# Three instead of two attention-output jobs behind the attention heads, in a single-core decoder block on Trainium2

## The chip, the cores and the metric

The kernel runs on one core of a Trainium2 chip. The metric is the device time of one execution, in microseconds (us), given as the median of several runs. The engines are named as in the profile: PE does matrix products, PEld loads their weights, DVE, ACT and POOL are the vector, scalar and general-purpose engines, SP issues most of the transfers.

## The reference

One decoder block over 2048 tokens of width 1024, in float32. What the change touches is the attention branch's output, its merge with the recurrent branch, and the last projection:

```python
h = rms_norm(x, g_norm[l]) * (1.0 + scale[:, None, :]) + shift[:, None, :]
proj = h @ w_in[l]
x_rnn, z_rnn, q, k, v, z_attn, g_r, g_a = jnp.split(proj, IN_SPLITS, axis=-1)
...
y_rnn = (hr * jax.nn.silu(z_rnn.astype(jnp.float32))).astype(dt) @ w_out_rnn[l]
...
o = dilated_attention_mixture(qh, kh, vh).reshape(B, S, D_ATTN)
y_attn = (o * jax.nn.silu(z_attn.astype(jnp.float32))).astype(dt) @ w_out_attn[l]
merged = jax.nn.sigmoid(g_r + bg_r) * y_rnn + jax.nn.sigmoid(g_a + bg_a) * y_attn
x = x + gate[:, None, :] * (merged @ w_o[l])
return rms_norm(x, g_final)
```

There are 8 heads of 128 channels. Attention is the mixture of three causal windows with dilations 1, 4 and 16.

## The kernel before

All products are made of pairs of float32r operands: a number is split into a high part (a copy, on ACT, `hi_act`) and a low part (the difference, on POOL or DVE, `lo_pool` and `lo_dve`), and `mm3` issues three matmuls for each product (high by high, high by low, low by high). The work goes through these stages:

1. The input projection and the recurrent branch, for the two halves of the sequence. Nothing of it changes. At its end the output weights are written to memory, once as split pairs (`wD`) and, for the attention weights, once unsplit (`wR`).
2. Attention. The sequence has four banks of 512 tokens. There are 16 "heads": the 8 heads for the first two banks, then the 8 heads for the last two. Each head has six units (`ORDER`), and one slot takes one unit through the engines by a written-out order (`plan`, `at`, `run`): scores of the slot's unit, softmax, and, seven slots later, transposes, and another slot later the sums with the values. A slot's work on the other engines is the softmax with its scaling (ACT and DVE), the splits of keys, queries, values (ACT high, POOL low) and of the transposed weights (ACT or DVE high, DVE low).
3. Between the parts of each slot a generator, `steps`, is advanced by `spend`. It makes the output products as eight jobs of 64 steps: jobs 0 to 3 multiply the recurrent branch (`yaT`) for banks 0 to 3, jobs 4 to 7 the attention branch (`oT`) for banks 0 to 3. A job has eight tiles (m), a tile has eight steps (k), and a step is one `mm3` on a 128x512 tile `pj`. How many steps a slot takes is `FILL`: 3.6 in the first half of the slots and 3.1 in the second, with `MORE` (0.8) in seven early slots. What is left after the last slot is issued at once.
4. The tail: the jobs at tile index `TAIL0` and above run behind the attention heads. Here the weights come unsplit from `wR` and are split as they come (`split_w`, high on ACT, low on DVE and POOL in turn); the first two halves still come as pairs. Beside these jobs `build_rows` makes the operands of the last projection from `w_o`, in four builds (k = 0 to 3), each at a written-out step of the tail: load two row blocks into the stage tiles st1 and st2, scale them with the gate (`gate_rows`, POOL), form the sums of a Strassen product (`combine`, DVE), and split them (`high` on ACT, `low` on DVE or POOL).
5. The last projection: eight pairs of seven products each, then the final norm. Its first pair reads only bank 0.

Each job's right-hand operand Y (eight 128x512 blocks) is loaded (`load_y`) into a ring of four R tiles and split (`split_y`) into yh and yl, nine of each, at steps given by `LOAD_Y` and `SPLIT_Y`. These count from the boundary of the jobs: step x belongs to the last tile of the job before for x = 0 to 7, and to the first tile of the job itself from 8 on, so that block k is needed at x = 8 + k. Each tile's result is multiplied with its merge gate, in jobs 4 to 7 added to the recurrent result, and stored (`load_g`, `evict`, `store`). The load of gates has a ring of four fg tiles, and every third tile of the tail uses s1 and s2.

With TAIL0 = 48 two jobs, 6 and 7, are in the tail. Job 6 reads bank 2, which the last heads write; its last block is taken from the last head's own tile, and three others through spare key tiles:

```python
if ys is oT and (n, k) == (2, KT - 1):
    Y0[False, n, k] = last_head[0].zt[:, 0].rearrange("p r j -> p (r j)")
    return
if ys is oT and n == 2 and k >= KH:
    t = T(ap_, [P, KQW], F32, "kraw", bufs=4)
    nc.sync.dma_start(t[:, :CH], ys[k * P : (k + 1) * P, n * CH : (n + 1) * CH])
    Y0[False, n, k] = t[:, :CH]
    return
```

Engines take their instructions in the order of the program, and so does each queue of transfers.

Of the kernel before, what the change touches and what calls it, by code (L numbers as in the profile page):

```python
# [10 lines left out]
F32 = mybir.dt.float32  # L11
# [9 lines left out]
P = 128  # L21
S = 2048
D = 1024
KT = D // P
NB = 4
CH = 512
# [5 lines left out]
BIG = 9984.0  # L32


FILL = (3.6, 3.1)
MORE = 0.8
NEG = 1e30

# [51 lines left out]
def decoder_block(ctx, tc, x, c, positions, g_norm, w_mod, b_mod, w_in, b_gate, conv_w, conv_b,  # L90
# [4 lines left out]
    def T(pool, shape, dt, tag, **kw):  # L95
        cnt[0] += 1
        return pool.tile(shape, dt, tag=tag, name=f"{tag}_{cnt[0]}", **kw)
# [1553 lines left out]
            at(e + 2, TAIL, self.store)  # L1651

    stored = set()
    TAIL0 = KT * (NB + 2)
    RAW = 2 * TAIL0 + 1


    def steps(jobs):

        tiles = [(j, m) for j in range(len(jobs)) for m in range(KT)]  # L1660
        Y, G = {}, {}

        def load_w(x):

            if x < 2 * len(tiles):
                assert x == n_w[0]
                j, m = tiles[x // 2]
                if x <= RAW:
                    load_wd(jobs[j][0], m, x % 2)
                    return  # L1670

                n_w[0] += 1
                i = (x - 2 * TAIL0) % 6
                W[x] = t = T(pS, [P, 2, KH, P], F32R, f"S{i}") if i < 4 else T(fp, [P, 2, KH, P], F32R, f"st{i - 1}")
                nc.sync.dma_start(t[:, 1].bitcast(F32), wR[m, x % 2])

        def split_w(x):
            if RAW < x < 2 * len(tiles):
                raw = W[x][:, 1].bitcast(F32)
                hi_act(W[x][:, 0], raw)  # L1680
                (lo_pool if x % 2 else lo_dve)(W[x][:, 1], raw, W[x][:, 0])

        def load_y(j, k):
            if j < len(jobs):
                w, ys, n = jobs[j]
                if ys is oT and (n, k) == (2, KT - 1):

                    Y0[False, n, k] = last_head[0].zt[:, 0].rearrange("p r j -> p (r j)")
                    return
                if ys is oT and n == 2 and k >= KH:  # L1690

                    t = T(ap_, [P, KQW], F32, "kraw", bufs=4)
                    nc.sync.dma_start(t[:, :CH], ys[k * P : (k + 1) * P, n * CH : (n + 1) * CH])
                    Y0[False, n, k] = t[:, :CH]
                    return
                assert ys is yaT or (n // 2, k, n % 2) in stored
                load_yd(ys, n, k)

        def split_y(j, k):
            if j < len(jobs):  # L1700
                Y[j, k] = yh, yl = [T(fl, [P, CH], F32R, tag, bufs=NY) for tag in ("yh", "yl")]
                w, ys, n = jobs[j]
                t = Y0.pop((ys is yaT, n, k))
                hi_act(yh[:], t[:])
                (lo_dve if k % 2 else lo_pool)(yl[:], t[:], yh[:])

        def load_g(t):
            j, m = tiles[t]
            w, ys, n = jobs[j]
            at_ = slice(m * P, (m + 1) * P), slice(n * CH, (n + 1) * CH)  # L1710
            G[t] = []
            for src in (grT,) if ys is yaT else (gaT, mrT):
                if t >= TAIL0 and (t - TAIL0) % 3 == 2 and t < TAIL0 + 13:
                    g = T(fp, [P, CH], F32, ("s1", "s2")[len(G[t])])
                else:
                    g = T(fl, [P, CH], F32, "fg", bufs=4)
                nc.sync.dma_start(g[:], src[at_])
                G[t].append(g)

        def evict(t, ps):  # L1720
            g = G[t]
            nc.vector.tensor_tensor(g[0][:], ps[:], g[0][:], ALU.mult)  # L1722
            if len(g) > 1:
                nc.vector.tensor_tensor(g[0][:], g[0][:], g[1][:], ALU.add)

        def store(t):
            j, m = tiles[t]
            w, ys, n = jobs[j]
            nc.sync.dma_start((mrT if ys is yaT else meT)[m * P : (m + 1) * P, n * CH : (n + 1) * CH], G.pop(t)[0][:])

        g_loads = {(0, 0): [0], (14, 0): [14], (15, 0): [15]}
        for x in range(13):
            g_loads[x, 3] = [x + 1]
        for k in range(KT):
            split_y(0, k)
        yield
        last = None
        for t, (j, m) in enumerate(tiles):
            ps = T(pj, [P, CH], F32, "pj")
            for k in range(KT):  # L1740
                x = 2 * t + k // KH
                if k % KH == 1:

                    if x < 2 * TAIL0:
                        load_w(x + 3)
                    for x1 in range(x + 3 if x == 2 * TAIL0 else x + 5, x + 6) if x >= 2 * TAIL0 else ():
                        load_w(x1)
                if k % KH == 2 and x >= 2 * TAIL0:
                    for x1 in (x + 2, x + 3) if x == 2 * TAIL0 + 1 else (x + 2,) if x == 2 * TAIL0 else (x + 3,):
                        split_w(x1)  # L1750
                if k == 1 and t:
                    evict(t - 1, last)
                if t < TAIL0:
                    if k == 3:
                        load_g(t)
                    if k == 7 and t:
                        store(t - 1)
                else:
                    if k == 4:
                        store(t - 1)  # L1760
                    for x in g_loads.pop((t - TAIL0, k), ()):
                        load_g(TAIL0 + x)
                wt = W[2 * t + k // KH]
                yh, yl = Y[j, k]
                mm3(ps[:], wt[:, 0, k % KH, :], wt[:, 1, k % KH, :], yh[:], yl[:], first=k == 0, last=k == KT - 1)
                if k % KH == KH - 1:
                    W.pop(2 * t + k // KH)


                x = m * KT + k - KT * (KT - 1)  # L1770
                j1 = j + 1
                if m == 0:
                    x, j1 = x + KT * KT, j

                if j1 == NB + 2:

                    if -14 <= x < KT - 14:
                        load_y(j1, x + 14)
                elif j1 and x in LOAD_Y:
                    load_y(j1, LOAD_Y[x])  # L1780
                if j1 and x in SPLIT_Y:
                    split_y(j1, SPLIT_Y[x])
                yield
            last = ps
        evict(len(tiles) - 1, last)
        store(len(tiles) - 1)
# [12 lines left out]
    LOAD_Y = {-12: 0, -10: 1, -8: 2, -6: 3, -2: 4, 4: 5, 5: 6, 6: 7}  # L1799
    SPLIT_Y = {-3: 0, 3: 1, 4: 2, 5: 3, 7: 4, 10: 5, 11: 6, 12: 7}  # L1800
    fill = steps([(0, yaT, n) for n in range(NB)] + [(1, oT, n) for n in range(NB)])
    next(fill)
    with tc.manual_schedule():
        units = []
        for g in range(2 * H):
            hd = Head(g // H, g % H)
            hd.enlist(NU * g)
            units += [(hd, u) for u in ORDER]
        last_head = [hd]
        owed = 0.0  # L1810
        first = min(s for s, _ in plan)
        end = max(s for s, _ in plan) + 1
        for s in range(first, max(end, len(units) + LAG + 1)):
# [22 lines left out]
                if evict:  # L1836
                    at(s + 1, HEAD, evict)
            run(s, TAIL)
        owed = spend(fill, (NB + 2) * KT * KT - n_steps[0], 0)
    pools.close("ap", "sc", "pT", "po")  # L1840

    fp = pools.open("fp", bufs=1)
# [9 lines left out]
    def on(n, fn, *args):  # L1852
        pend.setdefault(n, []).append((fn, args))
# [29 lines left out]
    def build_rows(s, k):  # L1883
        sub, add = ALU.subtract, ALU.add
        for d, fn, *args in (
            (0, gate_rows, k, 0), (4, gate_rows, k, 1), (5, high, "B11", k), (6, low, "B11", k, lo_dve),
            (9, combine, "T3", k, "B22", "B12", sub), (9, combine, "T2", k, "B11", "T3", add),
            (9, high, "B22", k), (9, high, "B21", k), (10, low, "B22", k, lo_pool), (10, low, "B21", k, lo_dve),
            (11, high, "T3", k), (11, high, "T2", k), (12, combine, "T4", k, "B21", "T2", sub), (12, low, "T3", k, lo_pool),
            (13, low, "T2", k, lo_dve), (13, high, "T4", k), (14, combine, "T1", k, "B22", "T2", sub),  # L1890
            (15, high, "T1", k), (15, low, "T4", k, lo_dve), (16, low, "T1", k, lo_pool)):
            on(s + d, fn, *args)

    A, ops = {}, {}
# [167 lines left out]
        on_p(n + 3, finish_row, p, 1)  # L2062
        fire_p()

    LAST = 2 * KT * KT
    with tc.manual_schedule():
        v["gate"] = stage(0, [P, D])
        nc.sync.dma_start(v["gate"][:], gateD[0:1, :].broadcast_to([P, D]))
        for k, x in enumerate((8, 32, 68, 92)):
            build_rows(x, k)  # L2070
            for i in range(2):
                on(max(x - 8 + 4 * i, 0), load_rows, k, i)
        on(107, load_left, 0, (0,))
# [58 lines left out]
```

## Time and profile before

| | |
|---|---|
| Median of 3 runs | 2251.11 us (2250.35 to 2255.52) |
| The profiled execution's own time | 2251.41 us |
| Its span, first to last instruction | 2249.6 us |
| Busy share of the span: PE, PEld, DVE, ACT, POOL | 97%, 82%, 64%, 57%, 48% |
| Mean granted PE clock | 0.988 |
| Memory traffic | 577.34 MB by transfers, mean 257 GB/s |

The span is shorter than the execution's time by 1.8 us. Busy time of PE counts a matmul from its start to its modelled end, which overlaps the next one, so that 97% is no measure of how densely it works; the distance between the starts of two matmuls is. The granted clock is 1.0 or 0.5 in any one moment, and a mean between them tells for what share of a stretch it was halved. Idle time of an engine is shown with what ended it.

### The profile page before, as it was taken

To read this page: it belongs to the slowest core of one execution; us is meant where nothing else is said; L and a number is where in the kernel's file an instruction comes from. 1 tells how busy PE (TensorE), PEld (TensorE's weight loads), DVE (VectorE), ACT (ScalarE), POOL (GpSimd) and SP (SyncE) were. 2 spreads that over 40 slices of the span, in tenths; PEclk is the share of its full clock that TensorE was granted. 3 is DMA by queue.
4 is the path that set the end of the run, shared out by engine and by line. 5 is a ranking of instruction groups with operands and counts; after the bars stand their busy time and mean duration, and the time that the engine had idled before them with its cause. 6 is when DMAs were issued, how large, how long until landed. Compare 5 with 4: busy or idle time off the path is not lost. (4 is left out here: it accounts for less than half of the span.)

```text
span 2249.6 us, 34130 instructions
## 1 busy us (share of the span) xinstructions
PE 2176.6 (97%) x11326; PEld 1840.2 (82%) x11326; DVE 1441.9 (64%) x2467; ACT 1282.6 (57%) x2554; POOL 1084.3 (48%) x799
## 2 busy tenths in 40 slices
PE   8999999999999999999999999999999998978998
PEld 4998888888778988888888877888888887856886
DVE  5838887878445815545445442566667776678787
ACT  5637678667533627556556203676778877433333
POOL 2557777767557422222222102555656655366443
PEclk9999999999999999999999999999999999988999
DMA  8367887887999378898999989988988877877543
GB/s 276 114 220 255 285 292 270 293 283 263 324 279 292 108 234 278 273 298 288 292 306 296 358 291 292 276 273 250 280 255 259 253 239 228 265 230 221 201 164 113
DMA packets 412133, 577.34 MB, mean 257 GB/s; under 512 B 72406, under 2 KB 270258, under 8 KB 410932
## 3 DMA queue, kind: packets, MB, share of 16 engines
q1 hardware_dynamic: 369748, 446.75, 63.9%
q10 hardware_dynamic: 42016, 128.36, 15.0%
q8 instruction: 90, 1.47, 0.3%
q14 instruction: 87, 0.71, 0.1%
q0 software_dynamic: 192, 0.05, 0.0%
HBM read 356.92 MB, written 218.11 MB: 256 GB/s over the span
## 5 line engine op out<-in xcount | busy, mean ns | idle before, releaser
L150 PE MATMUL pj<-yh,S 128*128 128x512 f32 x944 | 347.1, 410 | 22.6 <-DVE s L1722 6.5
L164 POOL TENSOR_TENSOR S<-R,S 128x512 fp32r<-128x512 f32 x168 | 256.8, 1536 | 175.1 <-ACT S L158 72.2
L150 PE MATMUL X<-T,S 128*128 128x512 f32 x1344 | 326.0, 392 | 5.0 <-ACT u L384 4.3
L150 PE MATMUL V<-T,S 128*128 128x512 f32 x1344 | 324.5, 390 | 1.2 <-DVE t L454 0.9
L150 PEld LDWEIGHTS X<-T,S 128*128 128x128 f32 x1344 | 252.8, 189 | 59.9 <-ACT u L384 5.5
L150 PEld LDWEIGHTS V<-T,S 128*128 128x128 f32 x1344 | 252.0, 188 | 55.4 <-DVE t L454 1.8
L150 PEld LDWEIGHTS pj<-yh,S 128*128 128x128 f32 x944 | 180.9, 192 | 60.2 <-ACT S L158 15.7
L150 PE MATMUL pj<-yl,S 128*128 128x512 f32 x472 | 188.8, 400 | 6.6 <-POOL yl L164 5.3
L164 POOL TENSOR_TENSOR S<-s,S 128x512 fp32r<-128x512 f32 x92 | 140.3, 1525 | 111.4 <-ACT S L158 65.4
L1421 ACT ACTIVATE pp<-pp,st 128x256 f32<-128x256 f32 (+3 forms) x256 | 133.8, 524 | 93.8 <-DVE st L1420 92.6
L150 PE MATMUL Z<-T,S 128*128 128x512 f32 x672 | 162.0, 390 | 0.0
L150 PE MATMUL Y<-T,S 128*128 128x512 f32 x672 | 161.8, 390 | 0.0
L150 PE MATMUL W<-T,S 128*128 128x512 f32 x672 | 161.7, 390 | 0.0
L150 PEld LDWEIGHTS W<-T,S 128*128 128x128 f32 x672 | 126.1, 188 | 26.9 <-issue 0.9
L150 PEld LDWEIGHTS Y<-T,S 128*128 128x128 f32 x672 | 126.0, 188 | 26.0
L150 PEld LDWEIGHTS Z<-T,S 128*128 128x128 f32 x672 | 125.9, 188 | 26.0
L167 DVE TENSOR_TENSOR ptl<-pT,pth 128x384 fp32r<-128x384 f32 (+1 forms) x160 | 97.9, 629 | 75.8 <-ACT pth L158 73.6
L164 POOL TENSOR_TENSOR s<-R,s 128x512 fp32r<-128x512 f32 x32 | 45.4, 1419 | 208.4 <-ACT s L158 160.8
L912 DVE SCALAR_TENSOR_TENSOR xc<-xr,par,xc 128x512 f32<-128x512 f32 x96 | 98.6, 1028 | 45.8 <-ACT xc L906 43.5
L158 ACT ACTIVATE S<-R 128x512 fp32r<-128x512 f32 x168 | 101.6, 622 | 46.3 <-DMA R<-in_w_in_dram 15.4
L1485 ACT ACTIVATE pp<-pp,M 128x256 f32<-128x256 f32 (+3 forms) x256 | 118.0, 523 | 10.0 <-DVE M L1608 10.0
L1420 DVE CUSTOM_DVE_ANT_0 pp<-sc,msk 128x256 f32<-128x256 f32 (+3 forms) x256 | 104.6, 449 | 23.9 <-PE sc L150 21.7
(407 smaller groups left out, 4940.7 us busy)
## 6 DMA issues: line engine op xcount, KB each, us to landing
sD<-S ACTq DMA_DIRECT2D x196, 512.0 KB, 4.2
S<-sD SPq DMA_DIRECT2D x196, 512.0 KB, 5.3
S<-wD SPq DMA_DIRECT2D x98, 512.0 KB, 5.5
R<-in_w_in_dram SPq DMA_DIRECT2D x136, 256.0 KB, 4.2
wD<-s ACTq DMA_DIRECT2D x64, 256.0 KB, 5.9
T<-in_w_mod_dram SPq DMA_DIRECT2D x8, 1024.0 KB, 11.7
vN<-ev SPq DMA_DIRECT2D x64, 128.0 KB, 2.8
zaT<-ev SPq DMA_DIRECT2D x32, 256.0 KB, 4.0
```

The source lines that it names most:

```text
L150: nc.tensor.matmul(o, lhsT=l, rhs=r, start=st, stop=sp, **kw)
L158: nc.scalar.activation(o, i, AF.Copy)
L164: nc.gpsimd.tensor_tensor(o, i, h.bitcast(F32), ALU.subtract)
L167: return nc.vector.tensor_tensor(o, i, h.bitcast(F32), ALU.subtract).ins
L912: nc.vector.scalar_tensor_tensor(xc, xr[:, i : i + CH], cw(i), xc, ALU.mult, ALU.add)
L1420: nc.vector.tensor_tensor_reduce(pdst, s_ps, mask, 1.0, 3e38, ALU.add, ALU.min, m_)
L1421: nc.scalar.activation(pdst, pdst, AF.Exp, bias=m_, scale=-1.0, accum_out=l_)
L1485: nc.scalar.activation(pp, pp, AF.Copy, scale=w)
```

## The change

- `TAIL0` goes from 48 to 40 tiles. Job 5 (attention output for bank 1, the second bank) moves behind the heads, and the tail has three jobs, 5, 6 and 7.
- `FILL` goes from (3.6, 3.1) to (2.85, 2.75) steps a slot.
- Within the tail the blocks k = 5 to 7 of the next job's Y go into the stage tiles st1 and st2 rather than the ring R, all three issued at x = -1, and the splits lie earlier (`LATE_LOAD_Y`, `LATE_SPLIT_Y`). The special sources for job 6 are gone.
- The four builds start at steps 8, 33, 78 and 142 of 192, rather than at 8, 32, 68 and 92 of 128, and one build spreads over 21 steps rather than 16, in another order. Its loads lie 7 and 4 steps ahead of it, rather than 8 and 4.
- The left operand of the last projection is loaded 20 steps ahead of the end of the tail, both halves together. The gates' tiles s1 and s2 are used to tile 20 of the tail.

```diff
-FILL = (3.6, 3.1)
+FILL = (2.85, 2.75)
...
-    TAIL0 = KT * (NB + 2)
+    TAIL0 = KT * (NB + 1)
...
-        def load_y(j, k):
+        def load_y(j, k, t):
             if j < len(jobs):
                 w, ys, n = jobs[j]
-                if ys is oT and (n, k) == (2, KT - 1):
-
-                    Y0[False, n, k] = last_head[0].zt[:, 0].rearrange("p r j -> p (r j)")
+                assert ys is yaT or (n // 2, k, n % 2) in stored
+                if t >= TAIL0 and k > 4:
+                    n_y[0] += 1
+                    i, half = divmod(k - 5, 2)
+                    if half == 0:
+                        v["y", j] = stage(1 + i, [P, D])
+                    Y0[False, n, k] = y = v["y", j][:, half * CH : (half + 1) * CH]
+                    nc.sync.dma_start(y, ys[k * P : (k + 1) * P, n * CH : (n + 1) * CH])
                     return
-                if ys is oT and n == 2 and k >= KH:
-
-                    t = T(ap_, [P, KQW], F32, "kraw", bufs=4)
-                    nc.sync.dma_start(t[:, :CH], ys[k * P : (k + 1) * P, n * CH : (n + 1) * CH])
-                    Y0[False, n, k] = t[:, :CH]
-                    return
-                assert ys is yaT or (n // 2, k, n % 2) in stored
                 load_yd(ys, n, k)
...
-                if t >= TAIL0 and (t - TAIL0) % 3 == 2 and t < TAIL0 + 13:
+                if t >= TAIL0 and (t - TAIL0) % 3 == 2 and t < TAIL0 + 21:
...
-        g_loads = {(0, 0): [0], (14, 0): [14], (15, 0): [15]}
-        for x in range(13):
+        g_loads = {(0, 0): [0], (23, 0): [23]}
+        for x in range(22):
             g_loads[x, 3] = [x + 1]
...
-                if j1 == NB + 2:
-
-                    if -14 <= x < KT - 14:
-                        load_y(j1, x + 14)
-                elif j1 and x in LOAD_Y:
-                    load_y(j1, LOAD_Y[x])
-                if j1 and x in SPLIT_Y:
-                    split_y(j1, SPLIT_Y[x])
+                for k1 in (LATE_LOAD_Y if t >= TAIL0 else LOAD_Y).get(x, ()) if j1 else ():
+                    load_y(j1, k1, t)
+                for k1 in (LATE_SPLIT_Y if t >= TAIL0 else SPLIT_Y).get(x, ()) if j1 else ():
+                    split_y(j1, k1)
...
+    LOAD_Y = {-12: [0], -10: [1], -8: [2], -6: [3], -2: [4], 4: [5], 5: [6], 6: [7]}
+    SPLIT_Y = {-3: [0], 3: [1], 4: [2], 5: [3], 7: [4], 10: [5], 11: [6], 12: [7]}
+    LATE_LOAD_Y = {-12: [0], -10: [1], -8: [2], -6: [3], -2: [4], -1: [5, 6, 7]}
+    LATE_SPLIT_Y = {-3: [0], 1: [1], 2: [2], 3: [3], 6: [4], 8: [5], 9: [6], 10: [7]}
...
-        owed = spend(fill, (NB + 2) * KT * KT - n_steps[0], 0)
+        owed = spend(fill, TAIL0 * KT - n_steps[0], 0)
...
-            (0, gate_rows, k, 0), (4, gate_rows, k, 1), (5, high, "B11", k), (6, low, "B11", k, lo_dve),
-            (9, combine, "T3", k, "B22", "B12", sub), (9, combine, "T2", k, "B11", "T3", add),
-            (9, high, "B22", k), (9, high, "B21", k), (10, low, "B22", k, lo_pool), (10, low, "B21", k, lo_dve),
-            (11, high, "T3", k), (11, high, "T2", k), (12, combine, "T4", k, "B21", "T2", sub), (12, low, "T3", k, lo_pool),
-            (13, low, "T2", k, lo_dve), (13, high, "T4", k), (14, combine, "T1", k, "B22", "T2", sub),
-            (15, high, "T1", k), (15, low, "T4", k, lo_dve), (16, low, "T1", k, lo_pool)):
+            (0, gate_rows, k, 0), (6, gate_rows, k, 1), (6, high, "B11", k), (7, low, "B11", k, lo_dve),
+            (12, combine, "T3", k, "B22", "B12", sub), (12, high, "B22", k), (13, combine, "T2", k, "B11", "T3", add),
+            (14, high, "B21", k), (14, low, "B22", k, lo_pool), (15, low, "B21", k, lo_dve), (15, high, "T3", k),
+            (16, high, "T2", k), (17, low, "T3", k, lo_pool), (17, combine, "T4", k, "B21", "T2", sub),
+            (18, low, "T2", k, lo_dve), (18, combine, "T1", k, "B22", "T2", sub),
+            (19, high, "T4", k), (20, high, "T1", k), (21, low, "T4", k, lo_dve), (21, low, "T1", k, lo_pool)):
...
-    LAST = 2 * KT * KT
+    LAST = 3 * KT * KT
...
-        for k, x in enumerate((8, 32, 68, 92)):
+        for k, x in enumerate((8, 33, 78, 142)):
             build_rows(x, k)
             for i in range(2):
-                on(max(x - 8 + 4 * i, 0), load_rows, k, i)
-        on(107, load_left, 0, (0,))
-        on(110, load_left, 0, (1,))
+                on(max(x - 7 + 3 * i, 2 * i), load_rows, k, i)
+        on(LAST - 20, load_left, 0)
```

More of the change, by code (lines that the diff above doesn't have):

```diff
@@ L1796, in spend @@
         return owed
-    LOAD_Y = {-12: 0, -10: 1, -8: 2, -6: 3, -2: 4, 4: 5, 5: 6, 6: 7}
-    SPLIT_Y = {-3: 0, 3: 1, 4: 2, 5: 3, 7: 4, 10: 5, 11: 6, 12: 7}
+    LOAD_Y = {-12: [0], -10: [1], -8: [2], -6: [3], -2: [4], 4: [5], 5: [6], 6: [7]}
+    SPLIT_Y = {-3: [0], 3: [1], 4: [2], 5: [3], 7: [4], 10: [5], 11: [6], 12: [7]}
+    LATE_LOAD_Y = {-12: [0], -10: [1], -8: [2], -6: [3], -2: [4], -1: [5, 6, 7]}
+    LATE_SPLIT_Y = {-3: [0], 1: [1], 2: [2], 3: [3], 6: [4], 8: [5], 9: [6], 10: [7]}
     fill = steps([(0, yaT, n) for n in range(NB)] + [(1, oT, n) for n in range(NB)])
@@ L1808, in decoder_block @@
             units += [(hd, u) for u in ORDER]
-        last_head = [hd]
         owed = 0.0
```

## The prediction

> **What bounds the kernel now.** I read the page first (busy shares), then the busy time of each engine in stretches cut at heads and at tail jobs, then PE's waits in the two regions, then single rows of the timelines.
>
> ```profile
> span 2249.6 us, 34130 instructions
> PE 2176.6 (97%) x11326; PEld 1840.2 (82%) x11326; DVE 1441.9 (64%) x2467; ACT 1282.6 (57%) x2554; POOL 1084.3 (48%) x799
> ```
>
> The stretches' columns are length, then busy time of PE, PEld, DVE, ACT, POOL with instruction counts, then granted clock, DMA share, GB/s. The first four are single heads, between the exchange matmuls of neighbours; then come attention, job 6, job 7 and the last projection.
>
> ```profile
> 1475.20:1505.20 30.00, 30.00 (x195) 26.78 (x194) 19.29 (x63) 21.14 (x68) 14.91 (x17) 1.00 0.84 253
> 1535.00:1571.80 36.80, 33.64 (x196) 29.29 (x196) 22.41 (x68) 24.72 (x76) 18.24 (x19) 0.91 0.80 247
> 1666.60:1699.80 33.20, 33.20 (x215) 29.91 (x214) 22.74 (x65) 28.08 (x72) 19.02 (x16) 1.00 0.87 267
> 1842.50:1886.90 44.40, 38.46 (x230) 32.91 (x230) 31.70 (x74) 32.42 (x80) 26.48 (x21) 0.96 0.76 234
> 1373.00:1962.00 589.00, 571.31 (x3552) 503.12 (x3553) 389.97 (x1064) 422.33 (x1150) 322.22 (x279) 0.99 0.84 259
> 1962.00:2028.30 66.30, 50.73 (x194) 38.90 (x193) 46.40 (x44) 22.30 (x38) 37.82 (x21) 0.90 0.76 236
> 2028.30:2087.80 59.50, 50.58 (x193) 38.77 (x192) 48.62 (x46) 18.87 (x33) 34.53 (x19) 0.89 0.70 222
> 2087.80:2249.60 161.80, 152.53 (x673) 126.03 (x672) 133.14 (x225) 57.01 (x115) 71.04 (x48) 0.98 0.46 155
> ```
>
> An undisturbed head takes 30.0 us in the first half and 33.2 in the second, with PE busy throughout: attention is bound by PE. A head that meets the boundary of two jobs takes longer: 36.8, and 44.4 with job 5's boundary in it. The tail jobs need as many matmuls as each other (some 194) and take 66.3 and 59.5 us. What they would take at PE's pace is read from the end of job 7, where nothing waits:
>
> ```profile
> 2084.00 0.39 PE L150 MATMUL pj<-yl,S 128*128 128x512 f32 x1
> ...
> 2087.40 0.39 PE L150 MATMUL pj<-yl,S 128*128 128x512 f32 x1
> ```
>
> The second matmul of a step comes five steps later after 3.40 us: 0.68 us a step, 43.5 us for a job of 64. So job 6 loses 66.3 - 43.5 = 22.8 us and job 7 16.0, together 38.8. The change adds no matmul and removes none; the time can move only by such losses.
>
> **Attention with fewer steps.** Slots run from -5 to 105: 60 at the first rate, 51 at the second, so the new rates give 60 x 2.85 + 7 x 0.8 + 51 x 2.75 = 316.9 of the 320 steps of jobs 0 to 4 (before, 379.7 of 384). The fill still ends with the heads, and 64 steps leave attention: **-43.5 us** while PE paces it. Does it still? A first-half head loses 6 x 0.75 x 0.68 = 3.1 us and becomes 26.9; against that stand ACT 21.1 (79%) and DVE 19.3 (72%). A second-half head loses 6 x 0.35 x 0.68 = 1.4 and becomes 31.8, with ACT 28.1 (88%) and DVE 22.7 (72%). No engine passes PE. Least slack is ACT's, and its idle time is not free:
>
> ```profile
> L1421 ACT ACTIVATE pp<-pp,st 128x256 f32<-128x256 f32 (+3 forms) x256 | 133.8, 524 | 93.8 <-DVE st L1420 92.6
> ```
>
> ACT's exponentials waited 92.6 us in all for DVE's row maxima, which wait for PE's scores. With shorter slots some of this turns into PE waiting. Bounds: nothing, since the second-half head ran at 28.08 of 33.20 without a loss, up to the whole second-half gain, 8 x 1.4 = 11.5 us. A gain isn't excluded, but counted under the boundaries. I take **+4**, nearer to nothing, because the share rises only from 85% to 88% and eight splits of yh leave ACT with job 5.
>
> PE's waits inside attention:
>
> ```profile
> PE pj L150 <- POOL yl L164: 5.1, 3, 3.1
> PE pj L150 <- ACT yh L158: 4.6, 3, 1.9
> PE sc L150 <- DVE st L1420: 3.1, 5, 1.5
> ```
>
> Most of it is the splitting of Y at boundaries, and job 5's is the worst of them:
>
> ```profile
> 1871.84 0.50 PE L150 MATMUL pj<-yh,S 128*128 128x512 f32 x1 [1.37 <-ACT yh L158]
> 1875.42 0.80 PE L150 MATMUL pj<-yl,S 128*128 128x512 f32 x1 [3.08 <-POOL yl L164]
> ...
> 1876.87 0.63 PE L150 MATMUL o<-pth,vh 128*128 128x256 f32 x2
> ```
>
> After the wait matmuls last longer (0.63 for two 256-wide ones, and the head's clock is 0.96): a wait of some microseconds costs again as half-clock time. This boundary leaves the heads: **-11.2** (44.4 less 33.2). At their end POOL and ACT have no more heads to serve and the loads have been asked for as before, but the last three blocks still go load, high, low through R, with four steps (2.7 us) between load and split, and a load takes longer:
>
> ```profile
> R<-oT SPq DMA_DIRECT2D x8, 256.0 KB, 6.4
> ```
>
> Nine steps lie between load and use, 6.1 us; with the load's 6.4 and two splits it is late by about 2: **+2** (bounds 0 and the 11.2). The four other boundaries stay where they are in steps, and a step lasts longer in time, so they can only relax: 0 here, up to -10 for the range (the 36.8 head lost 6.8 alone). Away from attention also go job 5's 16 weight loads, 8 Y loads, 16 gate loads and 8 stores on SP's queue; no attention row above waits for them, so nothing is counted.
>
> So the first tail job starts 48.7 us earlier, at about 1913.
>
> **The tail.** What PE waits for there now:
>
> ```profile
> PE pj L150 <- DVE s L1722: 6.5, 2, 4.5
> PE pj L150 <- DVE fg L1722: 5.9, 2, 5.4
> PE pj L150 <- ACT yh L158: 5.3, 3, 2.9
> PE pj L150 <- ACT T4h L158: 3.4, 1, 3.4
> ```
>
> L1722 is the eviction: DVE comes to it late, because the builds' sums and splits stand ahead of it, and PE has only two pj tiles. The clock at 0.90 and 0.89 adds 0.10 x 66.3 + 0.11 x 59.5 = 13.2 of the 38.8. DVE's and POOL's work (mean ns behind the busy time):
>
> ```profile
> L1722 DVE TENSOR_TENSOR fg<-pj,fg 128x512 f32<-128x512 f32 x13 | 8.9, 682 | 5.0 <-DMA fg<-gaT 3.6 <-PE pj L150 1.4
> L1724 DVE TENSOR_TENSOR fg<-fg,fg 128x512 f32<-128x512 f32 x13 | 14.6, 1123 | 0.8 <-DMA fg<-mrT 0.4
> L167 DVE TENSOR_TENSOR S<-S 128x512 fp32r<-128x512 f32 x10 | 12.7, 1272 | 12.1 <-ACT S L158 12.1
> L167 DVE TENSOR_TENSOR yl<-R,yh 128x512 fp32r<-128x512 f32 x6 | 7.4, 1248 | 6.4 <-ACT yh L158 6.4
> L1875 DVE TENSOR_TENSOR st<-st,st 128x512 f32<-128x512 f32 x12 | 14.8, 1233 | 0.1
> L167 DVE TENSOR_TENSOR B11l<-st,B11h 128x512 fp32r<-128x512 f32 x4 | 5.8, 1452 | 0.1
> L167 DVE TENSOR_TENSOR B21l<-st,B21h 128x512 fp32r<-128x512 f32 x4 | 6.0, 1499 | 0.0
> L167 DVE TENSOR_TENSOR T2l<-st,T2h 128x512 fp32r<-128x512 f32 x4 | 2.7, 684 | 0.0
> L167 DVE TENSOR_TENSOR T4l<-st,T4h 128x512 fp32r<-128x512 f32 x4 | 2.7, 682 | 0.0
> L1867 POOL TENSOR_TENSOR st<-st,st 128x1024 f32<-128x1024 f32 x8 | 21.2, 2661 | 5.9 <-DMA st<-in_w_o_dram 5.8
> L164 POOL TENSOR_TENSOR S<-S 128x512 fp32r<-128x512 f32 x10 | 16.7, 1672 | 11.1 <-ACT S L158 9.3 <-DVE fg L1722 1.8
> L164 POOL TENSOR_TENSOR yl<-R,yh 128x512 fp32r<-128x512 f32 x5 | 7.3, 1464 | 8.7 <-ACT yh L158 8.7
> L164 POOL TENSOR_TENSOR T1l<-st,T1h 128x512 fp32r<-128x512 f32 x4 | 5.1, 1282 | 11.6 <-ACT T1h L158 7.1 <-DMA st<-wR 4.5
> ```
>
> A job gives DVE 8 evictions, 8 additions, 8 weight splits and 4 splits of Y: 8 x 0.682 + 8 x 1.123 + 8 x 1.272 + 4 x 1.248 = 29.6 us. A build gives it four sums and four splits: 4 x 1.233 + 1.452 + 1.499 + 0.684 + 0.682 = 9.2. With two builds a job has 48.1 us of DVE in 43.5 of PE; that is both tail jobs now. With one it has 38.9. After the change job 5 has two builds (steps 8 to 29, 33 to 54), jobs 6 and 7 one each. POOL stays below: 8 x 1.672 + 4 x 1.464 for a job = 19.2 for a job, and 2 x 2.661 for the gates with three splits between 1.282 and 1.672, some 10, for a build: 39 us with two.
>
> Job 5: loss between 48.1 - 43.5 = 4.6 and job 6's 22.8. I take 13: the same work on DVE, but spread over 21 steps instead of 16, and no wait for the last head (below). Jobs 6 and 7: DVE no longer exceeds PE; loss between 0 and half of 16.0, as half of the builds are gone. I take 5 each, for one eviction behind a build's burst and the half clock after it. The tail becomes 3 x 43.5 + 13 + 5 + 5 = 153.5, against 125.8: **+27.7**.
>
> Edits with small prices. The special sources of job 6's Y go, and with them this wait:
>
> ```profile
> 1967.21 0.49 PE L150 MATMUL pj<-yh,S 128*128 128x512 f32 x1 [1.63 <-ACT yh L158]
> ```
>
> It is in job 6's 22.8, and a reason for my 13. Moved to the tail, job 5's weights come unsplit: 14 more highs on ACT, 7 lows each on DVE and POOL (counted above), and half the bytes. Added waits: Y's blocks 5 to 7 wait at step 55 on SP for build 1's last lows, issued at step 54, which is one POOL instruction of 1.28 to 1.67; behind them on SP stand weight halves that are five halves (20 steps, 13.6 us) ahead, so their cover hides it. If that is used up it costs those 1.7 us, and twice. `load_rows` for build 1 is now issued by ACT at steps 26 and 29, right behind build 0's last lows, so ACT stands for up to 1.7 us each, with the weight highs 12 steps (8.2 us) ahead behind it. ACT waited thus before, too, since its queue met T1l at the end of a build. Zero to 3, inside job 5's bounds. `load_left` and the last projection keep their distances: 161.8 us as before.
>
> The Trainium skill has a rule that speaks against bringing weight splits into the tail: "SBUF — State Buffer", section Who interferes with whom, states that a DVE instruction with two SBUF inputs and a GpSimd instruction that reads SBUF exclude each other for the whole instruction, so that every such split would go on one common bill of both engines. This trace agrees only nearly: alone such a DVE operation takes 0.68 and a POOL one 1.28, and where both are busy they take up to twice that in the means above, but they overlap in part. By the rule the bill of job 5 would be (20 + 16) x 0.68 + (12 + 6) x 1.28 + 4 x 2.66 = 58.2 us, a loss of 14.7 rather than my 13, and that of a job with one build 28 x 0.68 + 15 x 1.28 + 2 x 2.66 = 43.6, a loss of 0.1 rather than 5; the time would be 2222, an estimate by that page.
>
> **The sum.** 2251.4 (the profiled execution's own time, span 2249.6 and 1.8 around it) - 43.5 - 11.2 + 2 + 4 + 27.7 = 2230.4. The runs' median is 0.3 lower than that execution, so I predict 2230.1. A difference of 0.3%, 6.8 us, is about what a measurement of this kernel can tell from none.
>
> **The rivals.** *A, ACT paces the heads.* The second-half heads don't shrink (11.5) and the first-half ones by half (8 x 3.1 / 2 = 12.2), so 23.7 instead of 4: 2249.8. For it speaks the 92.6 us; against it, that PE lost nothing at 85%.
>
> *B, the loss belongs to the job, not to the builds: slower.* Weight splits, evictions and boundaries come with each job; if each of three tail jobs loses job 6's 22.8, the tail is 198.9, and the time 2275. It decides from a loss of 14.7 a job on (125.8 + 48.7 = 174.5 = 3 x 43.5 + 44). For it: job 7 lost 16.0 without the last head. Against: its largest waits were evictions and a T4h, all of builds.
>
> *C, the builds keep their loss.* The tail loses 38.8 as now, wherever the builds lie: 15.8 more, 2245.9.
>
> *D, more is won.* The four boundaries in attention relax by 10 and ACT costs nothing: 2216.
>
> That the fill does not end with the heads, so that the change wouldn't do what it says, the step count above excludes.
>
> **How the numbers follow.** Forecast 0.56, A 0.10, B 0.15, C 0.07, D 0.12. Forecast and D are faster, 0.68; A and C lie within 0.3%, 0.17; B is slower, 0.15. The range leaves out B and a part beyond D: from 2212 (D with another 4 of the tail's 23) to 2254 (A with 4 more in the tail).
>
> **What would show it.** Undisturbed heads of 26.9 and 31.8 us, without new PE waits for L1420 or pth; the first tail job near 1913; tail jobs of about 56, 48 and 48 us, with PE's waits for L1722 in job 5 alone and a clock near 1.0 in jobs 6 and 7. Heads of 29 and 33 us would make it wrong through A, a clock of 0.90 in all tail jobs through B.

## The result, and the profile after

The changed kernel takes 2245.14 us (median of 12 runs, 2240.74 to 2249.27), the kernel before 2253.06 on the same chip (12 runs). The ratio is 0.9966, with a 95% interval of 0.9957 to 0.9975: faster by 0.34%, some 8 us, where 21 were forecast. The profiled execution took 2247.45 us.

Its stretches, cut where the jobs begin; the columns are those of the prediction (length, busy time of PE, PEld, DVE, ACT, POOL, granted clock, DMA share, GB/s). They are attention to the start of job 5, then jobs 5, 6 and 7:

```profile
1373.00:1916.50 543.50, 528.03 (x3361) 465.73 (x3362) 374.56 (x1044) 414.94 (x1142) 313.96 (x275) 1.00 0.81 249
1916.50:1982.90 66.40, 50.22 (x193) 37.73 (x191) 44.99 (x42) 22.96 (x41) 36.39 (x22) 0.91 0.77 249
1982.90:2031.10 48.20, 47.54 (x193) 38.41 (x194) 36.01 (x38) 14.76 (x26) 25.23 (x16) 0.91 0.87 260
2031.10:2083.70 52.60, 47.80 (x194) 37.76 (x193) 36.70 (x40) 17.13 (x29) 26.53 (x16) 0.94 0.80 257
```

Attention ends 45.5 us earlier than before (589.0 to 543.5), and the tail takes 167.2 us where it took 125.8. A job that PE paces takes 43.5, so the three jobs lose 22.9, 4.7 and 9.1 us, together 36.7, where two jobs lost 38.8 before. The first tail job of the changed kernel is as long as the first tail job of the kernel before, 66.4 and 66.3. The last projection takes 162 us in both. So nearly everything that attention gave was spent in the tail, and most of the excess in job 5.

Single heads between exchange matmuls come next: one of the first half without a wait, the one that stands where the prediction's head of 33.2 stood, and the fourth of the second half, with the same head of the kernel before below it.

```profile
1582.60:1609.70 27.10, 27.10 (x180) 24.41 (x179) 19.24 (x62) 22.05 (x69) 17.66 (x17) 1.00 0.85 271
1638.50:1671.60 33.10, 32.58 (x209) 28.90 (x208) 25.18 (x67) 29.43 (x74) 22.35 (x19) 1.00 0.84 255
1740.70:1773.70 33.00, 33.00 (x222) 30.10 (x221) 24.15 (x66) 27.94 (x71) 19.50 (x17) 1.00 0.80 252
```

```profile
1772.10:1806.60 34.50, 34.50 (x227) 31.30 (x228) 26.60 (x68) 29.10 (x73) 20.51 (x16) 1.00 0.84 254
```

PE's waits in attention (us in total, times, longest), and below them the largest in job 5:

```profile
PE sc L150 <- POOL q L1382: 8.8, 10, 3.6
PE pT L1505 <- ACT pp L1485: 2.2, 6, 0.6
PE sc L150 <- DVE st L1420: 2.0, 3, 1.4
...
PE pj L150 <- DVE yl L167: 0.5, 1, 0.5
PE pj L150 <- POOL yl L164: 0.2, 1, 0.2
```

```profile
PE pj L150 <- DVE fg L1720: 12.2, 3, 7.2
```

The waits for split Y at the boundaries are nearly gone from attention (POOL yl was 5.1, ACT yh 4.6). What is new is a wait for q, the window queries that POOL casts at L1382; it was 1.3 us before.

The single wait of 7.2 us is near the start of job 5. It can be followed back by the timelines of PE, DVE, ACT and SP's queue:

```profile
1945.59 0.77 PE L150 MATMUL pj<-yh,S 128*128 128x512 f32 x1 [7.16 <-DVE fg L1720]
```

```profile
1931.54 2.48 DVE L1722 TENSOR_TENSOR fg<-fg,fg 128x512 f32<-128x512 f32 x1
1941.52 1.66 DVE L167 TENSOR_TENSOR S<-S 128x512 fp32r<-128x512 f32 x1 [7.51 <-ACT S L158]
1943.10 1.75 DVE L167 TENSOR_TENSOR B11l<-st,B11h 128x512 fp32r<-128x512 f32 x1
1944.77 0.68 DVE L1720 TENSOR_TENSOR fg<-pj,fg 128x512 f32<-128x512 f32 x1
```

```profile
1940.86 0.63 ACT L158 ACTIVATE S<-S 128x512 fp32r<-128x512 f32 x1 [10.55 <-DMA S<-wR]
```

```profile
1925.69 0.43 SPq L1715 DMA_DIRECT2D fg<-gaT  x1
1934.04 0.32 SPq L1715 DMA_DIRECT2D fg<-mrT  x1
1934.40 0.43 SPq L1727 DMA_DIRECT2D meT<-fg  x1
1934.88 0.43 SPq L1859 DMA_DIRECT2D st<-in_w_o_dram  x1
1935.41 0.92 SPq L1675 DMA_DIRECT2D S<-wR  x2
```

SP issues one gate load at 1925.69 and stands on the next until 1934.04. DVE's addition for the tail's first tile ends at 1931.54 + 2.48 = 1934.02, and only that frees an fg tile. Behind the waiting load stand the w_o rows and two weight halves. ACT gets its weights late, DVE waits 7.5 us for their high part, and behind that wait, in DVE's order, stand one low split of a build and then the eviction that PE needs. (An earlier gate load held SP too, from 1918.55 to 1923.43, until the addition for job 4's last tile.) The kernel before has the same picture at its first tail job, in SP's queue and on DVE:

```profile
1968.39 0.84 SPq L1717 DMA_DIRECT2D fg<-gaT  x1
1978.90 0.32 SPq L1717 DMA_DIRECT2D fg<-mrT  x1
```

```profile
1985.96 1.64 DVE L167 TENSOR_TENSOR S<-S 128x512 fp32r<-128x512 f32 x1 [7.08 <-ACT S L158]
1988.13 0.68 DVE L1722 TENSOR_TENSOR fg<-pj,fg 128x512 f32<-128x512 f32 x1
```

So two theories stood for job 5's 22.9 us: that they are its two builds on DVE ("builds", the prediction's), or that part of them is this entrance of the tail, which is there whatever is built ("entrance").

### The profile page after: what moved, and what is told of

Its sections match the earlier page's. It is cut to its first block, busy times and chain, and to the rows that moved or that the text cites. A ratio compares the mean times of both kernels' runs of the same rounds, so it can differ in the third digit from the quotient of the medians.

```text
span 2245.7 us, 34220 instructions
## 1 busy us (share of the span) xinstructions
PE 2177.2 (97%) x11326; PEld 1837.3 (82%) x11326; DVE 1446.2 (64%) x2475; ACT 1289.7 (57%) x2570; POOL 1087.1 (48%) x807
## 4 chain that ended last, share of the span: by engine, by line
PE 50%; DMA 8%; issue 4%; DVE 4%; POOL 3%; ACT 2%; SPq 2%; ACTq 0%; POOLq 0%; DVEq 0%
PE X L150 10%; PE V L150 9%; PE pj L150 7%; PE W L150 5%; PE Z L150 5%; PE Y L150 4%; PE sc L150 3%; PE o L150 3%; DMA R<-in_w_in_dram 1%; PE pg L150 1%; PE pT L1505 1%; DMA kraw<-kT 1%; PE pT L1518 1%; DMA S<-wR 1%; DMA kraw<-qT 1%
## 5 line engine op out<-in xcount | busy, mean ns | idle before, releaser
L150 PE MATMUL pj<-yh,S 128*128 128x512 f32 x896 | 330.8, 410 | 12.7 <-DVE fg L1720 7.2
L164 POOL TENSOR_TENSOR S<-R,S 128x512 fp32r<-128x512 f32 x168 | 251.9, 1507 | 175.8 <-ACT S L158 73.8
L150 PEld LDWEIGHTS pj<-yh,S 128*128 128x128 f32 x896 | 172.1, 192 | 46.5 <-issue 9.2
L150 PE MATMUL pj<-yl,S 128*128 128x512 f32 x448 | 179.7, 401 | 4.5 <-POOL yl L164 2.8
L150 PEld LDWEIGHTS Z<-T,S 128*128 128x128 f32 x672 | 125.8, 188 | 26.1
```

The source lines that it names most:

```text
L150: nc.tensor.matmul(o, lhsT=l, rhs=r, start=st, stop=sp, **kw)
L164: nc.gpsimd.tensor_tensor(o, i, h.bitcast(F32), ALU.subtract)
```

## The experiments

Ratios are against the kernel before, run on the same chip, with 95% intervals. The runs come from several chips, so an experiment is set beside the changed kernel by the two ratios (0.9966 for the changed kernel; 0.001 is 2.25 us). Job lengths come from one profiled execution each. Job 5 with nothing of the tail edited took 65.3 to 66.4 us in the profiles of the changed kernel, e4 and e5; job 7 is less steady, 49.7 to 52.6 in the same three.

**e1: the tail's second tile takes its gates into s1 and s2**, and every third from there, so that no gate load waits at the entrance.

```diff
-                if t >= TAIL0 and (t - TAIL0) % 3 == 2 and t < TAIL0 + 21:
+                if t >= TAIL0 and (t - TAIL0) % 3 == 1 and t < TAIL0 + 21:
...
-        g_loads = {(0, 0): [0], (23, 0): [23]}
-        for x in range(22):
+        g_loads = {(0, 0): [0], (22, 0): [22], (23, 0): [23]}
+        for x in range(21):
```

> Theory 'entrance': job 5's first stall comes from SP's queue, which stands on a gate load (fg<-mrT) of the tail's second tile until the addition of the tail's first tile frees an fg tile, with the weights and w_o rows behind it. Taking that wait away (s1 and s2 for the tail's second tile and every third from there) should remove PE's 7.2 us wait for L1720 and a half-clock stretch: job 5 from 66.4 to about 55, the time 8 to 12 us under the changed kernel's 2245, about 2235. Theory 'builds': job 5's loss is the DVE work of its two builds, so job 5 stays within 3 us of 66 and the time within 3 us of 2245.

Measured: 2238.77 us, ratio 0.9939 (0.9922 to 0.9956), by the ratios some 6 us less than the changed kernel. Job 5, PE's longest wait within it, and the two weight halves behind the gate loads on SP's queue:

```profile
1916.00:1976.90 60.90, 49.08 (x193) 37.50 (x192) 42.48 (x42) 22.97 (x41) 36.87 (x22) 0.94 0.82 273
```

```profile
PE pj L150 <- DVE s L1720: 2.1, 1, 2.1
```

```profile
1927.04 1.00 SPq L1675 DMA_DIRECT2D S<-wR  x2
```

The two weight halves that were issued at 1935.41 go out at 1927.04. The 7.2 us are gone, with 2.1 us for an eviction in their place, and job 5 is 5.5 us shorter, less than the 11 expected. "Builds" alone is out. The wait for an eviction at the very end of job 5, 4.7 us in the changed kernel, stays (5.0 here, at the first matmul of job 6).

**e2: the same edit on the kernel before.**

```diff
-                if t >= TAIL0 and (t - TAIL0) % 3 == 2 and t < TAIL0 + 13:
+                if t >= TAIL0 and (t - TAIL0) % 3 == 1 and t < TAIL0 + 13:
...
-        g_loads = {(0, 0): [0], (14, 0): [14], (15, 0): [15]}
-        for x in range(13):
+        g_loads = {(0, 0): [0], (13, 0): [13], (14, 0): [14], (15, 0): [15]}
+        for x in range(12):
```

> The same edit on the kernel before. Theory 'entrance': the first tail job there (job 6) had the same stall (5.4 and 2.0 us of PE waiting for L1722, after SP stood 10 us on fg<-mrT); it goes, job 6 falls from 66.3 to about 57, the time by 5 to 10 us, to about 2245. Theory 'builds': job 6 stays at 66, the time within 3 us of 2253.

Measured: 2248.52 us, ratio 0.9979 (0.9966 to 0.9991). Its first tail job falls from 66.3 to 58.2, as expected:

```profile
1962.00:2020.20 58.20, 49.79 (x194) 38.81 (x194) 45.02 (x43) 21.37 (x37) 36.27 (x20) 0.91 0.81 261
```

The median falls by 2.6 us only, less than the 5 expected. In the profiled execution job 7 grew from 59.5 to 62.1, which takes back part of it; why it grew is open. The 5.4 us wait is gone; of the two later waits for evictions in the job, 2.0 and 4.5 before, there are 4.4 and 1.9. The entrance is a cost of both kernels; the prediction had read it as builds.

**e3: build 1 moved from job 5 to job 6.**

```diff
-        for k, x in enumerate((8, 33, 78, 142)):
+        for k, x in enumerate((8, 72, 97, 142)):
```

> Build 1 moved from job 5 (step 33) to job 6 (step 72, with build 2 at 97), so that job 5 has one build and job 6 two. Theory 'builds': the loss goes with it, job 5 from 66 to about 50 and job 6 from 48 to about 60. Theory 'entrance': job 5 keeps its first stall (7.2 us and half clock) and loses only its last one (4.7 us and half clock), so about 58; job 6 gains about 7, to 55. The time near 2245 by both.

Measured: 2241.66 us, ratio 0.9965 (0.9950 to 0.9979), not to be told from the changed kernel's 0.9966. Jobs 5, 6 and 7:

```profile
1913.00:1970.90 57.90, 48.12 (x193) 37.41 (x192) 32.82 (x36) 17.89 (x31) 26.56 (x17) 0.91 0.85 266
1970.90:2028.10 57.20, 46.67 (x194) 36.76 (x192) 46.29 (x42) 23.26 (x41) 38.47 (x22) 0.97 0.81 258
2028.10:2077.30 49.20, 46.84 (x192) 37.67 (x193) 37.44 (x40) 13.98 (x24) 24.37 (x15) 0.93 0.79 250
```

Both theories hold a part. Job 5 loses 8.5 us with its second build and keeps its 7.1 us wait, as "entrance" had it (58). Job 6 gains 9.0. A job with two builds and no entrance loses 57.2 - 43.5 = 13.7; with one build and the entrance it loses 14.4; with one build and no entrance 4.7.

**e4: one of the two casts of the window queries on DVE.**

```diff
-                nc.gpsimd.tensor_copy(t[:, l], src.rearrange("p r (b a) -> p b r a", b=4))
+                (nc.vector if l else nc.gpsimd).tensor_copy(t[:, l], src.rearrange("p r (b a) -> p b r a", b=4))
```

> One of the two casts of the window queries (L1382) moved from POOL to DVE. If POOL's place in the order is what PE newly waits for in the heads (8.8 us for q, 1.3 before), the waits fall under 3 us and attention from 543.5 to about 537, the time by 5, to 2240. Rival: DVE's queue is as late as POOL's, the wait turns into one for DVE (q or the row maxima of L1420), attention stays within 2 us of 543.5 and the time at 2245.

Measured: 2304.16 us, ratio 1.0237 (1.0217 to 1.0257), and attention 601 us long: some 60 us slower than the changed kernel, where a gain of 5 or none was expected. DVE's wait, and PE's:

```profile
DVE q L1382 <- POOL kq L164: 53.7, 16, 4.5
```

```profile
PE sc L150 <- DVE st L1420: 43.8, 14, 6.7
```

The cast on DVE is that of the low parts, so it must follow POOL's low split of the keys and queries: DVE now stood 53.7 us on POOL, with the row maxima behind it, for which PE waited 43.8. It isn't the cast that is slow; what is ahead of it is late, and the wait had been carried to an engine that PE waits for in every slot.

**e5: the split of the last quarter of keys and queries earlier**, from the start of the head's first slot into the slot before, with its load one slot earlier.

```diff
-            for c, (ld, s, place) in enumerate(((5, 2, HEAD), (5, 2, SOFTMAX), (4, 1, HEAD), (3, 0, HEAD))):
+            for c, (ld, s, place) in enumerate(((5, 2, HEAD), (5, 2, SOFTMAX), (4, 1, HEAD), (4, 1, WEIGHTS))):
```

> The changed kernel, with the split of the keys' and queries' last quarter (c = 3) moved from the start of a head's first slot to the slot before (ACT's and POOL's place in the order; its load one slot earlier). Theory 'chain in one slot': that split (ACT), its low part (POOL) and the two window casts (POOL) have to fit between two slots' scores; in the shorter slots they no longer do, and PE waits for q (8.8 us, 1.3 in the kernel before). Then the waits fall under 3 us, attention from 543.5 to about 537 and the time from 2245 to about 2239. Rival: POOL is late for other reasons (values' splits ahead of it), the waits stay above 6 us and the time within 2 us of 2245.

Measured: 2240.39 us, ratio 0.9951 (0.9939 to 0.9963), by the ratios some 3.4 us less than the changed kernel, with intervals that still overlap; e10 and e9, on one chip, repeat the comparison. Attention and PE's waits in it:

```profile
1370.90:1910.80 539.90, 526.04 (x3360) 466.79 (x3361) 362.31 (x1044) 415.66 (x1142) 315.08 (x276) 0.99 0.81 251
```

```profile
PE sc L150 <- DVE st L1420: 6.1, 6, 2.1
PE sc L150 <- POOL q L1382: 3.2, 5, 1.1
```

The chain theory holds in the main: the waits for q fall from 8.8 to 3.2 and attention by 3.6 us, short of the 6.5 expected, as part of it comes back as a wait for DVE's row maxima (2.0 to 6.1).

**e6: e1, with DVE's eight instructions of a build spread evenly.**

```diff
-            (0, gate_rows, k, 0), (6, gate_rows, k, 1), (6, high, "B11", k), (7, low, "B11", k, lo_dve),
+            (0, gate_rows, k, 0), (4, gate_rows, k, 1), (5, high, "B11", k), (6, low, "B11", k, lo_dve),
...
-            (12, combine, "T3", k, "B22", "B12", sub), (12, high, "B22", k), (13, combine, "T2", k, "B11", "T3", add),
+            (9, combine, "T3", k, "B22", "B12", sub), (9, high, "B22", k), (11, combine, "T2", k, "B11", "T3", add),
...
-            (16, high, "T2", k), (17, low, "T3", k, lo_pool), (17, combine, "T4", k, "B21", "T2", sub),
+            (14, high, "T2", k), (15, low, "T3", k, lo_pool), (15, combine, "T4", k, "B21", "T2", sub),
...
```

> e1's gate tiles, and DVE's eight instructions of a build spread evenly from step 6 to 21 (sums at 9, 11, 15, 18, lows at 6, 13, 17, 21) in place of packed from 12 on. Theory 'burst': evictions are late because a build's DVE instructions come closer together than PE's steps; the wait of 5.0 us at the end of job 5 shrinks under 2, job 5 from 60.9 to about 55, the time from 2239 to about 2233. Rival 'total': DVE has 48 us of work in job 5 whatever the order; job 5 stays within 2 us of 60.9.

Measured: 2240.58 us, ratio 0.9943 (0.9928 to 0.9957), as e1. Job 5 takes 61.4. By the view of waits those for evictions are small now (at most 1.0), and another has come in their place:

```profile
PE pj L150 <- ACT T4h L158: 6.2, 2, 3.6
```

The name misleads. Here is the first of these two waits, with ACT and DVE just before its end:

```profile
1949.10 0.64 PE L150 MATMUL pj<-yh,S 128*128 128x512 f32 x1 [2.63 <-ACT T4h L158]
```

```profile
1948.38 0.63 ACT L158 ACTIVATE T4h<-st 128x512 fp32r<-128x512 f32 x1 [2.50 <-DVE st L1870]
```

```profile
1946.60 1.75 DVE L1870 TENSOR_TENSOR st<-st,st 128x512 f32<-128x512 f32 x1
1948.27 0.68 DVE L1720 TENSOR_TENSOR fg<-pj,fg 128x512 f32<-128x512 f32 x1
```

The matmul is the first of its tile, which needs a free pj tile, and the eviction on DVE ended at 1948.95, 0.15 us before it; T4h ended at 1949.01, by chance between the two. The 7.16 us wait of the changed kernel ended in the same way, 0.14 us behind its eviction (1945.45, 1945.59), and so did the other wait here (1972.00, 1972.15) and the 3.4 us under T4h in the kernel before (2074.16, 2074.31). So the two waits of e6 are for evictions, 2.6 and 3.6 us, and the first stands behind a sum of the build. "Burst" failed: spread evenly, the build's DVE work still holds evictions back, and the outcome is that of "total", 61.4 against 60.9. The wait at the very end of job 5 is small (0.6); two earlier ones are there instead.

**e7: the builds' order of before, 16 steps long, at the changed starts.**

```diff
-            (0, gate_rows, k, 0), (6, gate_rows, k, 1), (6, high, "B11", k), (7, low, "B11", k, lo_dve),
+            (0, gate_rows, k, 0), (4, gate_rows, k, 1), (5, high, "B11", k), (6, low, "B11", k, lo_dve),
...
```

> The changed kernel with the builds' 16-step order of before, at the changed starts (8, 33, 78, 142). If spreading a build over 21 steps saves anything, as the prediction's 13 for job 5 assumed, job 5 gets longer than 66.4, to about 72, and jobs 6 and 7 by 2 each; the time about 2253. If the order is worth nothing, job 5 stays within 3 us of 66 and the time within 3 us of 2245.

Measured: 2245.93 us, ratio 0.9972 (0.9963 to 0.9982). Jobs 5, 6 and 7:

```profile
1917.10:1980.10 63.00, 50.57 (x194) 39.11 (x193) 43.59 (x43) 21.60 (x37) 35.82 (x21) 0.89 0.78 251
1980.10:2033.50 53.40, 48.79 (x194) 37.77 (x193) 39.40 (x38) 18.58 (x31) 29.55 (x19) 0.94 0.83 263
2033.50:2084.90 51.40, 46.87 (x194) 36.76 (x193) 36.42 (x38) 15.32 (x26) 23.80 (x15) 0.97 0.78 248
```

Their sum, 167.8, is that of the changed kernel, 167.2. Job 5 is shorter by 3.4, job 6 longer by 5.2. Spreading a build over 21 steps saved nothing that these runs can tell.

**e8: the four builds in jobs 5 and 6, none in job 7.**

```diff
-        for k, x in enumerate((8, 33, 78, 142)):
+        for k, x in enumerate((8, 33, 72, 97)):
```

> The changed kernel with the four builds in two jobs, 5 and 6 (starts 8, 33, 72, 97), and none in job 7. If a second build in a job costs some 8.5 us more than a first one, job 6 goes from 48 to 57, job 7 from 52.6 to about 46, and the time is about 2248. If what counts is the sum of builds, job 6 rises as job 7 falls and the time stays at 2245. If three jobs are what saves the builds' loss, the tail gets 10 us longer, 2255.

Measured: 2252.58 us, ratio 1.0004 (0.9994 to 1.0014): without the third job for the builds the change gains nothing. Jobs 6 and 7:

```profile
1984.40:2043.00 58.60, 49.13 (x193) 38.51 (x193) 47.89 (x45) 21.46 (x39) 38.61 (x23) 0.91 0.79 252
2043.00:2090.20 47.20, 46.58 (x192) 37.65 (x193) 26.76 (x32) 9.69 (x16) 12.79 (x10) 0.93 0.78 240
```

A second build costs job 6 10.4 us; job 7, without its only build, is 2.0 shorter than in e3 and 5.4 shorter than in the changed kernel. The three jobs take 171.3 us, 4.1 more than in the changed kernel's profile; by the ratios the time is some 8.5 us longer, so about half of that is seen in the tail. The median lies between the 2248 and the 2255 of the two theories that had a cost.

**e9: e1, with all of job 5's weights loaded as split pairs.**

```diff
-    RAW = 2 * TAIL0 + 1
+    RAW = 2 * TAIL0 + 15
...
-                if x <= RAW:
+                if x <= 2 * TAIL0 + 1:
...
-                nc.sync.dma_start(t[:, 1].bitcast(F32), wR[m, x % 2])
+                if x <= RAW:
+                    nc.sync.dma_start(t[:].bitcast(F32), wD[jobs[j][0], m, x % 2])
+                else:
+                    nc.sync.dma_start(t[:, 1].bitcast(F32), wR[m, x % 2])
```

> e1's gate tiles, and all 16 weight halves of job 5 loaded as split pairs (512 KB each) in place of 14 unsplit ones (256 KB) split on the way: 7 lows less on DVE, 7 on POOL, 14 highs less on ACT, 3.7 MB more of transfers. Theory 'one order for splits and builds': job 5's loss of 17.4 comes from DVE, POOL and ACT carrying weight splits besides two builds; job 5 falls from 60.9 to about 51 (DVE 48 - 9 = 39 us of work), the time from 2239 to about 2230. Rival 'transfers': the larger loads come late, PE waits for S<-wD, job 5 stays at 60 or more.

Measured: 2232.42 us, ratio 0.9915 (0.9901 to 0.9928). Job 5:

```profile
1913.80:1970.30 56.50, 47.71 (x194) 36.55 (x193) 30.20 (x35) 13.53 (x23) 23.51 (x14) 0.97 0.98 348
```

DVE's time in it falls from 42.48 to 30.20, POOL's from 36.87 to 23.51, and the job from 60.9 to 56.5, less far than the 51 expected: 13.0 us are still lost in it. The transfers carry it: 348 GB/s, with 1.3 us of PE waiting for a pair.

**e10: e9 and e5 together, and e11: the weights of all three jobs as pairs** (`RAW = 2 * TAIL0 + 47`).

> e9 with e5's early split of the keys' last quarter. If the two are independent, e5's gain of 4 to 5 us comes on top of e9: about 2226. If e5's gain was drift, as e9.

> e10 with the weights of all three tail jobs as split pairs. By 'one order for splits and builds' jobs 6 and 7, which lose 5 each with one build, fall to about 45: 6 us less than e10, about 2220. By 'transfers', which have less slack there (Y, gates, w_o and 512 KB halves together), jobs 6 and 7 get longer, the time at or above e10's.

Measured: e10 2228.73 us, ratio 0.9898 (0.9883 to 0.9913); e11 2234.03, ratio 0.9920 (0.9907 to 0.9932). Attention takes 539.4 us in e10. Job 5 of e10, then job 7 of e11:

```profile
1911.10:1967.60 56.50, 47.89 (x193) 36.45 (x191) 32.42 (x35) 13.55 (x23) 22.59 (x14) 0.97 0.95 342
```

```profile
2019.10:2073.10 54.00, 47.88 (x194) 36.58 (x192) 25.11 (x32) 9.37 (x15) 13.84 (x9) 0.97 0.92 332
```

Below it PE's longest wait in e11's tail:

```profile
PE pj L150 <- ACT yh L158: 6.4, 3, 2.8
```

The gains of e5 and e9 add (e10 is 3.7 us below e9), and e10 is 1.0% faster than the kernel before and 0.7% faster than the changed one. In e11 PE waits 6.4 us for Y's high parts, which wait for their loads, as "transfers" had it; 2.4 of it falls in job 7, with 2.1 more for the pairs themselves. Job 7 is 6.5 us longer than e10's 47.5.

## Why the prediction was wrong, step by step

The prediction's profiled time was 2230.4 us, the profiled execution's 2247.45: 17.0 more. Attention gave 3.2 less than forecast, job 5 took 9.9 more, job 6 0.3 less, job 7 4.1 more; the sum is 16.9.

*Job 5: the step that failed.* "I take 13: the same work on DVE, but spread over 21 steps instead of 16, and no wait for the last head (below)." Measured 22.9, which is what the first tail job lost before (22.8). What was left out is the entrance of the tail. The 5.4 us that PE waited in the kernel before stood in the row of L1722, and the prediction put it down to "the builds' sums and splits" ahead of the eviction. What stood ahead was one weight split, late because SP stood on a gate load, and a single split of a build (0.7 us). e1 and e2 show it on both kernels (5.5 and 8.1 us of the job), and e3 by what a job with one build costs with the entrance and without it (57.9 in job 5, 48.2 in the changed kernel's job 6). SP's own waits in the kernel before tell it, and the prediction makes nothing of them:

```profile
SPq L1717 <- DVE fg L1724: 8.1, 2, 7.4
```

For two builds without the entrance 13 is the right size: job 6 loses 13.7 with two in e3 and 15.1 in e8. But the reasons given for 13 do not carry it. The spreading over 21 steps saved nothing in e7, and the wait for the last head was 1.6 us; so the agreement is luck. What the two builds' loss is made of is known in part: it goes through evictions that stand behind the builds' and the weights' splits on DVE (e6), and e9 takes 4.4 us of it away. The rest is open.

*Jobs 6 and 7: 5 each.* Job 6 lost 4.7, but not for the reason given. PE waits only 0.6 us within it. Its clock of 0.91, where the prediction looked for nearly 1.0, is one stretch of half clock at its start, behind the 4.7 us wait that ends job 5:

```profile
1982.90:1991.20 8.30, 7.64 (x17) 5.61 (x18) 8.27 (x8) 2.03 (x4) 5.33 (x4) 0.50 0.86 254
1991.20:2031.10 39.90, 39.90 (x177) 32.80 (x177) 27.74 (x31) 12.72 (x23) 19.89 (x12) 1.00 0.87 262
```

At half clock 8.3 us cost 4.15, so nearly all of job 6's loss comes from job 5's two builds (with build 1 moved, in e3, a wait of 4.7 us ends job 6 and none ends job 5), and the number is luck. Job 7 has what was forecast, one late eviction (2.2 us, under the name of T1h, 0.14 us behind the eviction's end), and besides it a wait of 1.8 for Y; a half-clock stretch of 3.4 us lies at each. So it lost 9.1 in the profiled execution. In e3, e4 and e5, whose job 7 is the same, it lost 5.7 to 6.7, in e4 and e5 with a clock of 1.00.

*Attention: -43.5, -11.2, +2, +4.* Together -48.7; measured -45.5. PE did pace the heads of the first half: the eight between their first and last exchange matmul fell from 253.6 to 227.6, 26.0 where 24.8 were forecast. The seven of the second half fell from 253.6 to 238.5, 15.1 where 9.8 and job 5's boundary, 11.2, were forecast. Where PE waits in neither kernel, a head shrank as forecast (34.5 to 33.0), but the head of 33.2 became 33.1 and not 31.8. The price of shorter slots was looked for on ACT; most of it that can be named came on POOL, as a chain between two slots (high part of the keys on ACT, low part and two casts on POOL), 8.8 us, and e5 takes 3.6 of it back. Where the second half's other microseconds went is open. The waits at the four boundaries did shrink, which was counted at 0.

*Rivals.* A's sign, heads of 33 us in the second half, showed in part, but not A's mechanism: PE's waits in attention are 8.8 us for POOL's q, and 2.2 for ACT's pp, and ACT was busy for 27.94 of 33.00 us in a head that lost nothing. C came nearest, with its time, 2245.9, and with a tail that loses 38.8, where 36.7 were measured. It said that the builds keep their loss wherever they lie; e8, with two in each of two jobs, loses 40.8, so that laying them apart saves 4.1 in the tail, where the forecast counted on 15.8. And part of C's 38.8 was the entrance, which neither had seen. B fell: jobs 6 and 7 lose far less than job 6 did before, though the clock stayed near 0.9 in them.

*The rule of the Trainium skill*, in "SBUF — State Buffer", section Who interferes with whom, gave 14.7 for two builds and 0.1 for one. The first lies near 13.7 and 15.1, but e9 speaks against it as the price of a job: seven splits fewer on each engine take 13.7 off the same bill, an estimate by that page of the Trainium skill, which leaves a loss of 1.0. Job 5 still lost 13.0 there. For one build 4.7 was measured, most of it the half clock behind job 5.

## What to carry to other kernels

A wait that the profile puts down to an eviction or another late instruction is to be followed up that engine's order, and where it leads to a load, on to the queue that issued it: one load that waits for a buffer holds back every load behind it. The name that a wait carries is itself to be tested by times: here several waits for evictions stood under names of ACT. Where a stage begins, its rotation of buffers is to be worked out against the last tiles of the stage before. An operand that is split on the way costs three engines' time; where the transfers still have room, as in e9 and no longer in e11, loading it split is the cheaper form.

## What the runs showed of the hardware that was not expected

Job 5 of e9 ran with transfers at 348 GB/s and a share of 0.98 of the DMA engines, and PE waited for a transfer of weights only 1.3 us, where the changed kernel's job 5 ran at 249. And the cost of one wait is more than its length: with PE's largest waits gone, the granted clock of job 5 rises from 0.91 (of 66.4 us) to 0.97 (of 56.5), so that 6.0 us lost to the half clock become 1.7. A wait need not be long for it: behind the 1.8 us wait in the changed kernel's job 7 a stretch of 3.4 us ran at 0.50.

```profile
2035.60:2039.00 3.40, 3.28 (x9) 2.08 (x8) 2.67 (x3) 2.42 (x4) 3.29 (x3) 0.50 1.02 329
```
